# Output projection of a decoder block: from sixteen row tiles of full products to seven block products for each pair of row tiles

## The chip, the core and the metric

The kernel runs on one core of one Trainium2 chip. The metric is the device time of one execution in microseconds; for the kernel before it is 2237.41 us, the median of 3 runs (2236.44 to 2240.11).

## What is computed

One decoder layer over 2048 positions of width 1024, all in float32: a conditioned RMS norm, a combined input projection, a recurrent branch, an attention branch with three dilated windows, two branch projections that are merged with sigmoid gates, and at the end

```python
    merged = jax.nn.sigmoid(g_r + bg_r) * y_rnn + jax.nn.sigmoid(g_a + bg_a) * y_attn
    x = x + gate[:, None, :] * (merged @ w_o[l])
return rms_norm(x, g_final)
```

The change is in the last of these: `merged` (2048 x 1024) times `w_o` (1024 x 1024), with the gate on its columns, the residual add and the final norm, and in what runs just ahead of it.

## The kernel before, in words

**Precision.** TensorE multiplies operands in a rounded float32 form. Each operand is therefore split into a high part, made by a copy on ScalarE (`hi_act`, L157), and a low part, the rest, made by a subtraction on GpSimd (`lo_pool`, L163) or VectorE (`lo_dve`, L166). One product is three matmuls (`mm3`: high x high, high x low, low x high, all recorded at L149). In names of tiles, an `h` or `l` at the end is the high or low part; a weight tile `S` holds both.

**Stages.** The input projection comes first. It is done in block form already: a pair of 2 x 2 blocks takes seven products instead of eight (`strassen`, with PSUM sums X, Z, W, V, Y; each product is 4 x 3 = 12 matmuls of 128x512). Attention follows, and under it, as filler, the two branch projections: a generator, `steps` (`fill`), goes through eight jobs, four for the recurrent branch and then four for the attention branch, numbered 0 to 7 here, each with 512 positions. A job has eight output tiles m, a tile has eight steps k, a step is one `mm3`. So a job is 64 steps, 192 matmuls.

**What a step issues.** At k = 1 and k = 5 `load_w` brings a weight tile S (four buffers, each for half of a tile's depth) three half tiles ahead of its use. At k = 1 VectorE also evicts the tile before (`evict`, L1711 and L1713: the sum in PSUM times the gate gaT, plus the other branch mrT). At k = 3 `load_g` loads gaT and mrT for this tile (tiles `fg`, four buffers, 256 KB each), and at k = 7 the tile before is stored to `meT`, which is `merged` turned. The next job's left side, eight pieces `y` of 256 KB, is loaded and split around the last tile of a job, at places that the tables `LOAD_Y` and `SPLIT_Y` give (buffers R, four).

**Weights.** Earlier in the kernel both branch weights are split once and put into a scratch tensor `wD`; a tile from there is 512 KB and ready to use (`load_wd`, L339).

**The last stretch.** Jobs 0 to 5 are spent under attention, in an order written out by hand (`manual_schedule`). Jobs 6 and 7 come after it, and the order there is not by hand: the scheduler of the framework places the instructions by itself. Job 6 runs first; then `output_operands` gates and splits `w_o` into `oh` and `ol`; then `output` is called for 16 row tiles of 128 positions, and beside each of the first eight rows eight steps of job 7 are emitted. From the third tile of job 6 on, `load_w` does not use `wD`: it loads the raw 256 KB (tile `wr`) and splits it there on ScalarE and on VectorE or GpSimd (L1670 ff.). A row loads x (`xo`) and its columns of `meT` (`mraw`), splits the latter (`mh`, `ml`), makes two halves of 8 x 3 = 24 matmuls in PSUM tiles `pq`, adds each half to x (L1851), squares the row on ScalarE (L1854), works out the reciprocal root on small operands (L170 to L179), scales (L1856) and stores 512 KB (L1857).

**Queues.** All loads and stores of this stretch are issued by SyncE, in program order. Its DMAs take turns on eight semaphores, so a DMA waits for the one that was issued eight before it.

Of the kernel before, what the change touches and what calls it, by code (L numbers as in the profile page):

```python
# [10 lines left out]
F32 = mybir.dt.float32  # L11
F32R = mybir.dt.float32r
# [8 lines left out]
P = 128  # L21
# [68 lines left out]
def decoder_block(ctx, tc, x, c, positions, g_norm, w_mod, b_mod, w_in, b_gate, conv_w, conv_b,  # L90
# [60 lines left out]
    def mm3(o, lh, ll, rh, rl, first=True, last=True, **kw):  # L151
        mm(o, lh, rh, first, False, **kw)
        mm(o, lh, rl, False, False, **kw)
        mm(o, ll, rh, False, last, **kw)

    def hi_act(o, i):
        nc.scalar.activation(o, i, AF.Copy)  # L157
# [7 lines left out]
    def lo_dve(o, i, h):  # L165
        return nc.vector.tensor_tensor(o, i, h.bitcast(F32), ALU.subtract).ins  # L166
# [168 lines left out]
    def load_wd(i, m, half):  # L335
        x = n_w[0]
        n_w[0] += 1
        W[x] = t = T(pS, [P, 2, KH, P], F32R, f"S{x % 4}")
        nc.sync.dma_start(t[:].bitcast(F32), wD[i, m, half])  # L339
# [1306 lines left out]
            at(e + 1, TAIL, self.merge, 3)  # L1646
            at(e + 2, TAIL, self.store)

    stored, whole = set(), []


    def steps(jobs):

        tiles = [(j, m) for j in range(len(jobs)) for m in range(KT)]
        Y, G = {}, {}

        def load_w(x):

            if x < 2 * len(tiles):
                assert x == n_w[0]  # L1660
                j, m = tiles[x // 2]
# [4 lines left out]
                n_w[0] += 1  # L1666
                W[x] = T(pS, [P, 2, KH, P], F32R, f"S{x % 4}")
                t = T(whole[0], [P, KH, P], F32, "wr", bufs=3)
                rows = slice(x % 2 * KH * P, (x % 2 + 1) * KH * P)
                nc.sync.dma_start(t[:], (w_out_rnn, w_out_attn)[jobs[j][0]][0, rows, m * P : (m + 1) * P]  # L1670
                                  .rearrange("(k p) m -> p k m", p=P))
# [36 lines left out]

        def evict(t, ps):
            g = G[t]  # L1710
            nc.vector.tensor_tensor(g[0][:], ps[:], g[0][:], ALU.mult)  # L1711
            if len(g) > 1:
                nc.vector.tensor_tensor(g[0][:], g[0][:], g[1][:], ALU.add)  # L1713
# [99 lines left out]
    pools.close("ap", "sc", "pT", "po")  # L1813

    fp = pools.open("fp", bufs=1)
    whole.append(pools.open("wr", bufs=1))
    pq = pools.open("pq", bufs=4, space=PSUM)
    oh = T(fp, [P, KT, D], F32R, "oh")
    ol = T(fp, [P, KT, D], F32R, "ol")
    gf = T(fp, [P, D], F32, "gf")  # L1820
    nc.sync.dma_start(gf[:], g_final.unsqueeze(0).broadcast_to([P, D]))
    gate_b = T(fp, [P, D], F32, "gate_b")
    nc.sync.dma_start(gate_b[:], gateD[0:1, :].broadcast_to([P, D]))

    def output_operands():
        for k in range(KT):
            t = T(fp, [P, D], F32, "xo", bufs=2)
            nc.sync.dma_start(t[:], w_o[0, k * P : (k + 1) * P, :])
            nc.vector.tensor_tensor(t[:], t[:], gate_b[:], ALU.mult)
            hi_act(oh[:, k, :], t[:])  # L1830
            (lo_dve if k % 2 else lo_pool)(ol[:, k, :], t[:], oh[:, k, :])

    def output(n):

        for r in range(4):
            xo = T(fp, [P, D], F32, "xo", bufs=2)
            nc.sync.dma_start(xo[:], xv[n, r])
            t = T(fp, [P, KT, P], F32, "mraw", bufs=2)
            c0 = n * CH + r * P
            nc.sync.dma_start(t[:], meT[:, c0 : c0 + P].rearrange("(k p) j -> p k j", p=P))  # L1840
            th = T(fp, [P, KT, P], F32R, "mh", bufs=3)
            tl = T(fp, [P, KT, P], F32R, "ml", bufs=3)
            hi_act(th[:], t[:])
            lo_dve(tl[:], t[:], th[:])
            for q in range(2):
                cq = slice(q * CH, (q + 1) * CH)
                ps = T(pq, [P, CH], F32, "pq")
                for k in range(KT):
                    mm3(ps[:], th[:, k, :], tl[:, k, :], oh[:, k, cq], ol[:, k, cq],
                        first=k == 0, last=k == KT - 1)  # L1850
                nc.vector.tensor_tensor(xo[:, cq], ps[:], xo[:, cq], ALU.add)  # L1851
            ob = T(fp, [P, D], F32, "ob", bufs=1)
            ss = T(fp, [P, 3, 1], F32, "ss", bufs=4)
            nc.scalar.activation(ob[:], xo[:], AF.Square, accum_out=ss[:, 0])  # L1854
            rstd(ss)
            nc.vector.scalar_tensor_tensor(ob[:], xo[:], ss[:, 1], gf[:], ALU.mult, ALU.mult)  # L1856
            nc.sync.dma_start(outv[n, r], ob[:])  # L1857
            yield
# [9 lines left out]
    pools.close("wr", "fp", "pq", "fl", "pR", "pS", "pjb")  # L1868


# [27 lines left out]
```

## Time and profile before

| | us |
|---|---|
| median of 3 runs | 2237.41 |
| the profiled execution | 2235.07 |
| its span, first to last instruction | 2233.3 |
| TensorE busy | 2185.9 (98%) |
| VectorE / ScalarE / GpSimd busy | 1348.6 / 1256.2 / 978.3 |
| mean granted TensorE clock | 0.994 |
| DMA, mean over the span | 257 GB/s |

A line of an operation names the source line, the engine, the output and the inputs with their shapes, the count, and after the bar the busy time in us and the mean ns of one. The mean of a 128x512 matmul (390 ns) is longer than the distance between two of them, because they overlap; the pace has to be read from the chain of waits, where runs of matmuls stand with their count. A line of a window gives, for a stretch of the span, the busy time of each engine with its count of instructions, the granted clock, the share of time in which the DMA engines were busy, and GB/s.

### The profile page before, as it was taken

The page shows a single profiled execution, that of the slowest core. Times are in us where ns is not written, and L with a number is a line of the kernel's source. Part 1 is how long each engine was busy: PE and PEld are TensorE (multiplying, and loading weights), DVE is VectorE, ACT ScalarE, POOL GpSimd, SP SyncE. Part 2 cuts the span into 40 slices and gives each one's busy share as a digit, 9 for nine tenths or more (in the row PEclk, how much of TensorE's full clock was granted, in tenths as well). Part 3 has the DMA queues.
Part 4 walks back from the last instruction along what each step waited for, and adds up shares of the span by engine and source line. Part 5 has one row for each costly group of instructions (what it writes and reads, how often), then busy time and mean ns, then how long its engine had stood idle before and what let it go on. Part 6 is the DMA issues. An engine that isn't in the chain of part 4 may idle for free.

```text
span 2233.3 us, 33998 instructions
## 1 busy us (share of the span) xinstructions
PE 2185.9 (98%) x11422; PEld 1851.1 (83%) x11422; DVE 1348.6 (60%) x2380; ACT 1256.2 (56%) x2481; POOL 978.3 (44%) x734
## 2 busy tenths in 40 slices
PE   8999999999999999999999999999999998999998
PEld 5998888888778998888888887888888887878886
DVE  5838887878455815544545442566677777666443
ACT  6638678668543627556556202667778887533211
POOL 2457777767557422222222102455566665332100
PEclk9999999999999999999999999999999999999999
DMA  8367887887998378888888988988988887899542
GB/s 286 117 211 259 287 295 269 292 282 269 326 282 288 114 229 271 286 286 280 287 288 278 343 291 286 285 265 259 271 255 264 246 262 216 254 338 284 155 132 85
DMA packets 428626, 573.64 MB, mean 257 GB/s; under 512 B 72134, under 2 KB 292514, under 8 KB 427428
## 3 DMA queue, kind: packets, MB, share of 16 engines
q1 hardware_dynamic: 390612, 451.73, 64.9%
q10 hardware_dynamic: 37648, 119.70, 14.0%
q8 instruction: 90, 1.47, 0.3%
q14 instruction: 84, 0.69, 0.1%
q0 software_dynamic: 192, 0.05, 0.0%
HBM read 357.44 MB, written 213.91 MB: 256 GB/s over the span
## 4 chain that ended last, share of the span: by engine, by line
PE 55%; DMA 6%; DVE 3%; ACT 3%; issue 2%; POOL 2%; SPq 1%; ACTq 0%; POOLq 0%; DVEq 0%
PE pj L149 11%; PE X L149 8%; PE V L149 7%; PE pq L149 7%; PE sc L149 4%; PE W L149 4%; PE Z L149 4%; PE o L149 4%; PE Y L149 3%; PE pT L1501 1%; DMA R<-in_w_in_dram 1%; PE pg L149 1%; PE pT L1514 1%; POOL S L163 1%; DMA gaT<-ev 1%
## 5 line engine op out<-in xcount | busy, mean ns | idle before, releaser
L149 PE MATMUL pj<-yh,S 128*128 128x512 f32 x1024 | 367.8, 403 | 9.7 <-ACT yh L157 4.8
L163 POOL TENSOR_TENSOR S<-R,S 128x512 fp32r<-128x512 f32 x168 | 252.2, 1509 | 175.0 <-ACT S L157 64.9
L149 PE MATMUL V<-T,S 128*128 128x512 f32 x1344 | 324.6, 390 | 3.7 <-DVE t L450 3.5
L149 PE MATMUL X<-T,S 128*128 128x512 f32 x1344 | 324.5, 390 | 2.9 <-POOL S L163 1.9
L149 PEld LDWEIGHTS V<-T,S 128*128 128x128 f32 x1344 | 251.8, 188 | 58.4 <-DVE t L450 2.4
L149 PEld LDWEIGHTS X<-T,S 128*128 128x128 f32 x1344 | 251.4, 188 | 58.0 <-POOL S L163 2.8
L149 PEld LDWEIGHTS pj<-yh,S 128*128 128x128 f32 x1024 | 193.2, 189 | 47.8 <-ACT yh L157 6.7
L149 PE MATMUL pj<-yl,S 128*128 128x512 f32 x512 | 201.6, 394 | 6.2 <-POOL yl L163 5.1
L1417 ACT ACTIVATE pp<-pp,st 128x256 f32<-128x256 f32 (+3 forms) x256 | 133.8, 524 | 94.0 <-DVE st L1416 92.9
L163 POOL TENSOR_TENSOR S<-s,S 128x512 fp32r<-128x512 f32 x84 | 128.9, 1535 | 113.5 <-ACT S L157 68.8
L149 PE MATMUL Z<-T,S 128*128 128x512 f32 x672 | 162.0, 390 | 0.0
L149 PE MATMUL Y<-T,S 128*128 128x512 f32 x672 | 161.8, 390 | 0.0
L149 PE MATMUL W<-T,S 128*128 128x512 f32 x672 | 161.6, 389 | 0.0
L149 PEld LDWEIGHTS W<-T,S 128*128 128x128 f32 x672 | 126.0, 188 | 26.9 <-issue 0.9
L149 PEld LDWEIGHTS Y<-T,S 128*128 128x128 f32 x672 | 125.9, 188 | 26.0
L149 PEld LDWEIGHTS Z<-T,S 128*128 128x128 f32 x672 | 125.9, 188 | 26.1
L166 DVE TENSOR_TENSOR ptl<-pT,pth 128x384 fp32r<-128x384 f32 (+1 forms) x160 | 97.9, 629 | 75.6 <-ACT pth L157 73.4
L163 POOL TENSOR_TENSOR s<-R,s 128x512 fp32r<-128x512 f32 x32 | 45.9, 1434 | 198.4 <-ACT s L157 172.1
L157 ACT ACTIVATE S<-R 128x512 fp32r<-128x512 f32 x168 | 101.7, 621 | 48.1 <-DMA R<-in_w_in_dram 21.1
L908 DVE SCALAR_TENSOR_TENSOR xc<-xr,par,xc 128x512 f32<-128x512 f32 x96 | 98.5, 1026 | 45.7 <-ACT xc L902 43.5
L1481 ACT ACTIVATE pp<-pp,M 128x256 f32<-128x256 f32 (+3 forms) x256 | 118.0, 523 | 9.9 <-DVE M L1604 9.9
L1416 DVE CUSTOM_DVE_ANT_0 pp<-sc,msk 128x256 f32<-128x256 f32 (+3 forms) x256 | 104.6, 449 | 23.6 <-PE sc L149 21.3
(334 smaller groups left out, 4731.3 us busy)
## 6 DMA issues: line engine op xcount, KB each, us to landing
sD<-S ACTq DMA_DIRECT2D x196, 512.0 KB, 4.1
S<-sD SPq DMA_DIRECT2D x196, 512.0 KB, 5.0
S<-wD SPq DMA_DIRECT2D x100, 512.0 KB, 5.4
R<-in_w_in_dram SPq DMA_DIRECT2D x136, 256.0 KB, 4.3
wD<-s ACTq DMA_DIRECT2D x64, 256.0 KB, 5.0
T<-in_w_mod_dram SPq DMA_DIRECT2D x8, 1024.0 KB, 12.0
vN<-ev SPq DMA_DIRECT2D x64, 128.0 KB, 2.7
zaT<-ev SPq DMA_DIRECT2D x32, 256.0 KB, 4.4
```

The costliest lines, as they stand in the source:

```text
L149: nc.tensor.matmul(o, lhsT=l, rhs=r, start=st, stop=sp, **kw)
L157: nc.scalar.activation(o, i, AF.Copy)
L163: nc.gpsimd.tensor_tensor(o, i, h.bitcast(F32), ALU.subtract)
L166: return nc.vector.tensor_tensor(o, i, h.bitcast(F32), ALU.subtract).ins
L908: nc.vector.scalar_tensor_tensor(xc, xr[:, i : i + CH], cw(i), xc, ALU.mult, ALU.add)
L1416: nc.vector.tensor_tensor_reduce(pdst, s_ps, mask, 1.0, 3e38, ALU.add, ALU.min, m_)
L1417: nc.scalar.activation(pdst, pdst, AF.Exp, bias=m_, scale=-1.0, accum_out=l_)
L1481: nc.scalar.activation(pp, pp, AF.Copy, scale=w)
L1501: nc.tensor.transpose(pt[:, c0 + j * P : c0 + (j + 1) * P], pp[i][:, k * P : (k + 1) * P], ident)
L1514: nc.tensor.transpose(pt[:, c * P : (c + 1) * P], pp[:, half * P : (half + 1) * P], ident)
```

## The change

`load_w` always loads the split tile from `wD`, also in jobs 6 and 7:

```diff
-                if not whole or j == NB + 2 and m < 2:
-                    load_wd(jobs[j][0], m, x % 2)
-                    return
...
-                hi_act(W[x][:, 0], t[:])
-                (lo_dve if x % 2 else lo_pool)(W[x][:, 1], t[:], W[x][:, 0])
+                load_wd(jobs[j][0], m, x % 2)
```

The output projection is written in block form. Two row tiles of 128 positions, cut into two halves of the depth, stand against `w_o` cut into 2 x 2 blocks of 512 x 512. Seven right operands (`B11`, `T2`, `T3`, `T1`, `B21`, `T4`, `B22`, each 4 x 128x512, high and low) are built once from the gated rows of `w_o`; `build_rows(s, k)` spreads this, for one of four depth pieces k, over the steps s to s + 19 of jobs 6 and 7. Per piece: two gatings of 128x1024 on GpSimd, four differences on VectorE, seven high parts on ScalarE, four low parts on VectorE and three on GpSimd.

```diff
-    spend(fill, KT * KT, 0)
-    output_operands()
-    for n in range(NB):
-        for _ in output(n):
-            for _ in range(KT):
-                next(fill, None)
+    with tc.manual_schedule():
+        v["gate"] = stage(0, [P, D])
+        nc.sync.dma_start(v["gate"][:], gateD[0:1, :].broadcast_to([P, D]))
+        load_rows(0)
+        for k in range(KH):
+            build_rows((8, 32, 72, 96)[k], k)
+            if k:
+                on((16, 44, 75)[k - 1], load_rows, k)
+        on(LAST - 24, load_left, 0)
...
+        for s in range(LAST):
+            next(fill)
+            fire(s)
...
+        load_rows_x(0)
+        load_rows_x(1)
+        nc.sync.dma_start(v["gf"][:], g_final.unsqueeze(0).broadcast_to([P, D]))
+        fire_p()
+        for p in range(NP):
+            output_pair(p)
```

`LAST` is 128: jobs 6 and 7 now run through without a break, all 384 matmuls, and then come eight pairs p of seven products. `load_rows(k)` brings two 512 KB rows of `w_o` into two of five staging tiles; `gateD` is another 512 KB. For each pair, `load_left` brings two 512 KB tiles of `meT`, `left_events` make four sums and differences on VectorE and seven split operands (ScalarE; four low parts on VectorE, three on GpSimd), four products ahead of their use. `output_pair` writes the products in this order, with their sums:

```diff
+        product(p, 0, X, "B11", True, False)
+            last_output(p - 1)
+        product(p, 1, Z, "T2", True, True)
+        product(p, 2, W_, "T3", True, True)
+        product(p, 3, V, "T1", True, False)
+            product(p, 4, X, "B21", False, True)
+        product(p, 5, Y, "T4", True, True)
```

`last_output` is the seventh product (`B22`, on V). A product is 12 matmuls. VectorE makes u2 = Z + X and u3 = W + u2 and the four sums with x from PSUM, GpSimd adds u2 and u3 to x in three pieces, and each row is squared, scaled and stored as before, some products later. In the last pair the product with `T4` comes ahead of that with `B21`, the first row is squared in two halves, and its two halves of 256 KB are scaled and stored by ScalarE and by VectorE with SyncE. The whole stretch, from the start of job 6 to the end, is in an order written by hand.

More of the change, by code (lines that the diff above doesn't have):

```diff
@@ L1833, in output @@
[L1833 to L1858, printed above, removed]
@@ L1861, in decoder_block, with stage @@
-    spend(fill, KT * KT, 0)
-    output_operands()
-    for n in range(NB):
-        for _ in output(n):
-            for _ in range(KT):
-                next(fill, None)
-    pools.close("wr", "fp", "pq", "fl", "pR", "pS", "pjb")
+    px_ = pools.open("px", bufs=1, space=PSUM)
+    for name in ("B11", "T2", "T3", "T1", "B21", "T4", "B22"):
+        B[name] = [T(fp, [P, KH, CH], F32R, name + l) for l in "hl"]
+    def stage(i, shape, dt=F32):
+        return T(fp, shape, dt, f"st{i}")
+    pend = {}
@@ new lines, in on, with fire, load_rows, gate_rows @@
+    def on(n, fn, *args):
+        pend.setdefault(n, []).append((fn, args))
+    def fire(n):
+        for fn, args in pend.pop(n, ()):
+            fn(*args)
+    v = {}
+    tt = nc.vector.tensor_tensor
+    def load_rows(k):
+        for i in range(2):
+            v[k, i] = t = stage(1 + i + 2 * (k % 2), [P, D])
+            nc.sync.dma_start(t[:], w_o[0, (k + i * KH) * P : (k + i * KH + 1) * P, :])
+    def gate_rows(k, i):
+        nc.gpsimd.tensor_tensor(v[k, i][:], v[k, i][:], v["gate"][:], ALU.mult)
@@ new lines, in part, with difference, high @@
+    def part(name, k):
+        name = {"T3": "B12", "T4": "B21"}.get(name, name)
+        if name[0] == "T":
+            if (name, k) not in v:
+                v[name, k] = T(fp, [P, KH, P], F32, {"T1": "s1", "T2": "s2"}[name])
+            return v[name, k][:].rearrange("p k j -> p (k j)")
+        i, j = int(name[1]) - 1, int(name[2]) - 1
+        return v[k, i][:, j * CH : (j + 1) * CH]
+    def difference(name, k, a, b):
+        tt(part(name, k), part(a, k), part(b, k), ALU.subtract)
+    def high(name, k):
+        hi_act(B[name][0][:, k, :], part(name, k))
@@ new lines, in decoder_block, with load_left, left @@
+    A, ops = {}, {}
+    NP = 2 * NB
+    def load_left(p):
+        for half in range(2):
+            shape = [P, KH, 2 * P]
+            A[p, half] = t = T(up[0], shape, F32, f"A{half}", bufs=2) if p else stage(1 + half, shape)
+            nc.sync.dma_start(t[:], meT[half * KH * P : (half + 1) * KH * P, p * 2 * P : (p + 1) * 2 * P]
+                              .rearrange("(k p) j -> p k j", p=P))
+    def left(p, name):
+        if name in ("s1", "s2"):
+            return v[name][:]
+        i, j = int(name[1]) - 1, int(name[2]) - 1
+        return A[p, j][:, :, i * P : (i + 1) * P]
@@ new lines, in left_sum, with left_split @@
+    def left_sum(p, dst, a, b, op):
+        if dst[0] == "s" and (dst, p) not in v:
+            v[dst, p] = v[dst] = T(fp, [P, KH, P], F32, dst)
+        tt(left(p, dst), left(p, a), left(p, b), op)
+    def left_split(p, i, name):
+        x = 7 * p + i
+        r = x % 7
+        t = T(pS, [P, 2, KH, P], F32R, f"S{r - 3}") if r > 2 else stage((3, 4, 0)[r], [P, 2, KH, P], F32R)
+        ops[x] = t
+        hi_act(t[:, 0], left(p, name))
+        (lo_pool if i % 2 else lo_dve)(t[:, 1], left(p, name), t[:, 0])
@@ new lines, in decoder_block, with load_rows_x, cols, square @@
+    XO, SS = {}, {}
+    def load_rows_x(p):
+        n, r = divmod(2 * p, 4)
+        for i in range(2):
+            XO[p, i] = t = T(up[0], [P, D], F32, "xo", bufs=4)
+            nc.sync.dma_start(t[:], xv[n, r + i])
+    def cols(p, i, j):
+        return XO[p, i][:, j * CH : (j + 1) * CH]
+    def square(p, i, js=(0, 2)):
+        if (p, i) not in SS:
+            SS[p, i] = T(up[0], [P, 3, 1], F32, "ss", bufs=4)
+        jk = T(up[0], [P, D], BF16, "jk", bufs=1)
+        c = slice(js[0] * CH, js[1] * CH)
+        nc.scalar.activation(jk[:, c], XO[p, i][:, c], AF.Square, accum_out=SS[p, i][:, 2 if js == (0, 1) else 0])
@@ new lines, in finish_row, with product @@
+    def finish_row(p, i, last=True):
+        n, r = divmod(2 * p, 4)
+        ss, t = SS.pop((p, i)), XO.pop((p, i))
+        if last:
+            rstd_last(ss)
+        nc.vector.scalar_tensor_tensor(t[:], t[:], ss[:, 1], v["gf"][:], ALU.mult, ALU.mult)
+        nc.sync.dma_start(outv[n, r + i], t[:])
+    up, n_p, psum = [], [0], {}
+    def product(p, i, ps, b, first, last):
+        bh, bl = B[b]
+        s = ops.pop(7 * p + i)
+        for k in range(KH):
+            mm3(ps[:], s[:, 0, k, :], s[:, 1, k, :], bh[:, k, :], bl[:, k, :],
+                first=first and k == 0, last=last and k == KH - 1, skip_group_check=True)
+        n_p[0] += 1
```

157 lines of the change are left out of this document (135 added, 22 removed).

## The prediction, made blind

> **What bounds the kernel now.** I read the page's first part, then the chain of waits from its end backwards, then windows over the last stretch.
>
> ```profile
> PE 2185.9 (98%) x11422; PEld 1851.1 (83%) x11422; DVE 1348.6 (60%) x2380; ACT 1256.2 (56%) x2481; POOL 978.3 (44%) x734
> ```
>
> TensorE sets the span. What counts is the pace of its matmuls, and the chain gives it:
>
> ```profile
> 1004.85 2.72 PE X L149 x12
> ...
> 2132.52 5.44 PE pj L149 x24
> 2137.96 87.05 PE pq L149 x384
> ...
> 2225.03 0.70 DVE xo L1851
> ...
> 2225.81 1.16 ACT ob L1854 x2
> ...
> 2228.38 1.28 DVE ob L1856
> ```
>
> (The first row is of the chain in the block products of the input projection, asked for by itself; the others are of the last 100 us.) 384 matmuls in 87.05 us are 226.7 ns each; a block product of 12 takes 2.72 us, the same pace. The last matmul is issued out by 2225.0; the tail to the span's end, 2233.3, is 8.3 us.
>
> ```profile
> 1950.00:2050.00 100.00, 96.42 (x423) 77.95 (x423) 69.82 (x79) 38.06 (x55) 37.52 (x22) 1.00 0.99 314
> 2060.00:2225.00 165.00, 165.00 (x728) 136.32 (x727) 64.21 (x132) 29.55 (x52) 7.07 (x3) 1.00 0.41 134
> ```
>
> So the last stretch (jobs 6 and 7 and the output) has two parts: up to 2050 TensorE loses 3.6 us while the DMA engines are busy 0.99 of the time, and after it TensorE has no gap and DMA is at 0.41. What it waits for in the first part is DMA, one transfer behind the other:
>
> ```profile
> 1956.77 6.92 DMA S<-wD
> ...
> 1963.76 7.16 DMA fg<-mrT
> ...
> 1970.96 7.01 DMA xo<-in_w_o_dram
> ```
>
> The stretch has 2 x 192 matmuls of the jobs and 16 x 48 = 768 of the output, 1152 in all: 1152 x 0.2267 = 261.2 us, with the 3.6 us 264.8 us. Counted back from 2225.0 it begins near 1960.
>
> **The change, part by part.**
>
> *Products.* 8 pairs x 7 x 12 = 672 matmuls take the place of 768. At 226.7 ns the 96 are worth 21.8 us, and all of it is on the path. The stretch's floor becomes 1056 x 0.2267 = 239.4 us.
>
> *DMA beside jobs 6 and 7.* This is the term that decides. Before, job 7 was spread between output rows, so its loads had 24 + 48 matmuls to hide under; and most weight tiles were 256 KB. Now both jobs run through: 384 x 0.2267 = 87.1 us. In this time must land: 30 of the 32 weight tiles of 512 KB (two are on their way), 32 loads of gaT and mrT and 16 stores of 256 KB, 8 pieces y of job 7 of 256 KB, 8 rows of `w_o` and the gate of 512 KB, and two left tiles of 512 KB. That is 15360 + 8192 + 4096 + 2048 + 4096 + 512 + 1024 = 35328 KB, 36.2 MB; in 87.1 us, 415 GB/s. What DMA has reached when it was busy all the time:
>
> ```profile
> 1260.00:1270.00 10.00, 9.68 (x43) 7.71 (x42) 5.24 (x10) 2.85 (x5) 0.85 (x1) 1.00 1.04 396
> 1270.00:1280.00 10.00, 10.00 (x45) 8.26 (x45) 6.94 (x9) 1.14 (x3) 4.23 (x4) 1.00 1.02 399
> ...
> 1930.00:1940.00 10.00, 10.00 (x67) 8.86 (x66) 6.66 (x10) 4.84 (x10) 3.23 (x2) 1.00 1.02 346
> 1940.00:1950.00 10.00, 10.00 (x68) 9.05 (x67) 4.88 (x8) 4.11 (x8) 3.83 (x3) 1.00 1.03 337
> 1960.00:1970.00 10.00, 8.82 (x39) 6.90 (x38) 3.00 (x4) 0.00 (x0) 1.16 (x1) 1.00 1.02 383
> 1970.00:1980.00 10.00, 7.99 (x35) 5.97 (x34) 4.43 (x5) 3.70 (x5) 3.39 (x3) 1.00 1.08 349
> ```
>
> None reaches 415, so TensorE must wait for bytes. 399 is a window that consists nearly of large reads; 314 is the mean of 1950 to 2050 above, with small runs in it. The four windows between have just these loads, weight tiles, y, gaT, mrT and stores, and their mean is 354. I take 355: 36.2 MB / 355 GB/s = 102 us, **+14.9 us** of waiting. Bounds: 399 gives 90.7 us, +3.6; 314 gives 115.3 us, +28.2.
>
> Where it shows: a weight tile is asked for when its buffer is free, three half tiles (3 x 2.72 = 8.2 us) ahead of use. Rows of issues, the last number being the us to landing:
>
> ```profile
> S<-wD SPq DMA_DIRECT2D x100, 512.0 KB, 5.4
> ...
> fg<-mrT SPq DMA_DIRECT2D x32, 256.0 KB, 5.2
> ...
> R<-oT SPq DMA_DIRECT2D x28, 256.0 KB, 6.2
> ...
> xo<-in_w_o_dram SPq DMA_DIRECT2D x8, 512.0 KB, 5.8
> ```
>
> 5.4 us leave 2.8 us of room, which is two 512 KB transfers ahead in the queue (1.5 us each at 355 GB/s). The first weight tile behind the gate and two rows of `w_o` has three ahead; so has the one at step 44 with two rows and a y. The last pieces y are loaded 9 steps (6.1 us) ahead of use, and landing alone is 6.2. These three places should show stalls of 2 to 4 us; they are how the 14.9 us appear, not more on top. SyncE is in order too: mrT takes the buffer that VectorE's second addition frees, so its load waits there, with weight tile and store queued behind.
>
> *Splits taken out.* 28 raw weight tiles go, and the output's own operands:
>
> ```profile
> L157 ACT ACTIVATE S<-wr 128x512 fp32r<-128x512 f32 x22 | 13.7, 628 | 30.7 <-DMA wr<-in_w_out_attn_dram 21.3 <-PE pj L149 9.1
> ...
> L163 POOL TENSOR_TENSOR S<-wr,S 128x512 fp32r<-128x512 f32 x11 | 17.2, 1565 | 40.6 <-ACT S L157 40.5
> L163 POOL TENSOR_TENSOR ol<-xo,oh 128x1024 fp32r<-128x1024 f32 x4 | 10.2, 2553 | 15.7 <-ACT oh L157 13.0 <-issue 2.7
> ...
> L166 DVE TENSOR_TENSOR S<-wr,S 128x512 fp32r<-128x512 f32 x11 | 10.9, 997 | 2.7 <-ACT S L157 2.7
> L1713 DVE TENSOR_TENSOR fg<-fg,fg 128x512 f32<-128x512 f32 x12 | 10.7, 891 | 7.6 <-DMA fg<-mrT 7.6
> L1711 DVE TENSOR_TENSOR fg<-pj,fg 128x512 f32<-128x512 f32 x12 | 8.2, 683 | 3.4 <-DMA meT<-fg 1.7 <-DMA fg<-gaT 0.9 <-PE pj L149 0.8
> ```
>
> None of these engines sets the end, so I credit nothing beyond the old 3.6 us.
>
> *Right operands built.* ScalarE 28 x 0.63 = 18 us, VectorE 16 x 0.89 + 16 x 1.0 = 30 us, GpSimd 12 x 1.57 + 8 x 2.55 = 39 us, beside 102 us. With the evictions, 16 x (0.68 + 0.89) = 25 us, VectorE is at 55 of 102. I cost it at nothing: the cover is the matmuls of both jobs, the last piece is done by step 115 of 128. Without cover one piece would add about 20 steps, 13.6 us.
>
> *Start of the products.* Four x rows, the final weights and the second pair's two left tiles, 3584 KB = 3.7 MB, are issued only after the last store of job 7: eviction 1.6 us, 10.3 us at 355 GB/s, 2 us to land, then on VectorE a sum, and a split, 0.89 + 0.63 + 1.0: 16.4 us. The second pair's first operand is needed after six products, 6 x 2.72 = 16.3 us. **+1 us**, between 0 and 4.
>
> *Products after that.* VectorE has per pair four sums, four low parts, six evictions, two scalings and small operations (1.4 us per row, between the chain's 1.16 and 1.28 rows): 3.6 + 4.0 + 4.1 + 2.6 + 2.8 = 17.1 us of 7 x 2.72 = 19.0. Off the path, with two products of slack in every PSUM sum: 0. At a tenth more it still fits.
>
> *Clock.* A long wait lowers the granted clock:
>
> ```profile
> 1866.87 0.50 PE L149 MATMUL pj<-yh,S 128*128 128x512 f32 x1 [1.35 <-ACT yh L157]
> 1870.44 0.79 PE L149 MATMUL pj<-yl,S 128*128 128x512 f32 x1 [3.08 <-POOL yl L163]
> ```
>
> ```profile
> 1870.00:1880.00 10.00, 9.55 (x44) 8.65 (x45) 4.28 (x9) 3.44 (x11) 3.42 (x3) 0.68 0.32 104
> ```
>
> After these two the clock was 0.68 over 10 us, 3.2 us lost; in 1970 to 1980, with 2.0 us of shorter gaps, it stayed at 1.00. One or two of the stalls above are of the long kind, partly inside DMA waiting anyway: **+2 us**, between 0 and 6. The Trainium skill, "TensorE: Matmul & The Clock Gate", Part 1, has the clock halve after an idle window of about 3.4 us; by it stalls of 2 to 3 us would cost nothing and this term would be 0. The trace is against it as a threshold: a gap of 3.08 us was enough here.
>
> *Tail.* The last row is squared in two halves and scaled in halves on two engines: from 1.16 and 1.28 us about 0.35 and 0.6 go, the last store is 256 KB instead of 512 KB (0.4 less at most), one small addition comes in: **-1.1 us**, between -2 and 0. The other row's scaling (1.28 us) and two 128x512 operations lie under the last product, 2.72 us.
>
> *Sum.* 239.4 + 14.9 + 1 + 2 = 257.3 us for 264.8: -7.5; with the tail, and a rounding up for restarts after gaps (0.11 us each in the 0.50 row, some ten): -7.4. From the profiled 2235.07 that is 2227.7 us. The profiled execution lies 2.34 us under the median, so for the median **2230 us**.
>
> **The rivals.**
>
> *Slower, by DMA.* If the stage gets the 314 GB/s of 1950 to 2050, jobs 6 and 7 take 115.3 us; with 3 us at the start of the products and 5 us of clock: 239.4 + 28.2 + 8 = 275.6, +10.8, with the tail +9.7: 2247 us. It decides against the change below 330 GB/s (109.7 us). For it: stores and loads mixed, and DMA behind in-order waits of SyncE. Against: the windows of the same mix at 337 to 383, though only one of them is below 346.
>
> *No wall.* At the 399 of the best window, 90.7 us, nothing at the start and no long stall: 239.4 + 3.6 = 243.0, -21.8, with the tail -22.9: 2214 us. For it: nearly half the bytes are 512 KB weight tiles and rows, as in that window. Against: half are not. The Trainium skill, "HBM Reference", Specifications, says that a core streaming alone measures about 425 GB/s; no window here shows that, the best being 399. By it the 36.2 MB would take about 85 us, an estimate from that page, and there would be no wait at all.
>
> *VectorE binds the products.* If contention makes its 17.1 us per pair 20, each pair gains 1 us: +8 us, 2238 us. For it: it is in order, and holds left operands, evictions and rows. Against: uncontended 128x512 operations are 0.68 to 0.70.
>
> **How the numbers follow.** Forecast (337 to 385 GB/s) 0.55; slower by DMA 0.22; no wall 0.12; VectorE 0.11. Such a measurement tells about 0.2% (4.5 us) from no change. Faster by more: rates above about 344 GB/s, most of the forecast and the second rival, 0.59. Within: rates from 319 to 344 and most of the third, 0.21. Slower: 0.20. The range is 2219 (385 GB/s, nothing lost elsewhere) to 2243 (320 GB/s); about one in ten lies on either side.
>
> **What would show it.** In the profile after: 24 matmuls of a job in well over 5.44 us, DMA share near 1 and 340 to 370 GB/s for about 100 us from 1960; stalls behind `S<-wD` near the first `w_o` rows and at step 44, and at the last y pieces of job 7; then eight pairs at 19.0 us without gaps; a tail of about 7 us. It is wrong if job time is 87 us, if the products show waits on VectorE or GpSimd, or if DMA is below 0.95 while TensorE waits (then it is SyncE's order, not bytes).

## The result, and the profile after

The changed kernel takes 2241.53 us (median of 20 runs, 2235.32 to 2246.81), the kernel before beside it on the same chip 2237.30 us (20 runs). The ratio is 1.0018, 95% interval 1.0011 to 1.0025: 4.2 us slower where 7.4 us faster was forecast. The profiled execution took 2239.79 us, its span is 2238.0.

The page of the changed kernel answers the line of the engines first:

```profile
PE 2171.1 (97%) x11326; PEld 1834.1 (82%) x11326; DVE 1403.2 (63%) x2452; ACT 1267.8 (57%) x2524; POOL 1054.7 (47%) x784
```

96 matmuls are gone, as planned, and TensorE is busy 14.8 us less. Its span is longer all the same, so idle time took their place. Windows over the stretch show where: first the kernel before, cut where its last matmul of job 7 ends, then the changed kernel, cut at the same event (columns: window, length, busy time and count of TensorE, its weight loads, VectorE, ScalarE, GpSimd, then granted clock, DMA share, GB/s).

```profile
1958.70:2105.00 146.30, 142.72 (x624) 116.15 (x623) 88.71 (x122) 47.19 (x71) 41.48 (x23) 1.00 0.85 271
2105.00:2225.00 120.00, 120.00 (x530) 99.06 (x528) 45.97 (x96) 19.47 (x35) 0.75 (x1) 1.00 0.36 117
```

```profile
1961.00:2074.30 113.30, 96.11 (x385) 74.20 (x383) 57.78 (x74) 23.86 (x39) 44.97 (x26) 0.94 0.91 322
2074.30:2228.70 154.40, 153.11 (x673) 125.74 (x671) 129.06 (x214) 53.78 (x108) 70.17 (x47) 1.00 0.45 158
```

Before, jobs 6 and 7 were spread among 240 matmuls of the output: 146.3 us, with a loss of 3.6 us. Now they run through. Their 384 matmuls need 384 x 226.7 ns = 87.1 us and take 113.7 (1960.8 to 2074.5, by the first and last matmul). The products after them take 154.2 us for a floor of 672 x 226.7 ns = 152.3, and the tail from the last matmul to the end is 9.3 us for 8.3. In all 277.2 us stand against 266.5 + 8.3 = 274.8: +2.4 us. (The rest of the difference between the two spans lies ahead of job 6, where both kernels issue the same instructions; that start falls anywhere between 1957 and 1968 us in the profiles of this study, so I compare lengths of stages, not spans.)

The 26.6 us lost in the jobs are of two kinds: TensorE is idle for 113.3 - 96.1 = 17.2 us of the window, and busy for 96.1 us where 87.1 would do. The waits of TensorE in the jobs (what waited, for what: us in total, times, longest):

```profile
PE pj L149 <- DMA S<-wD: 10.2, 4, 5.2
PE pj L149 <- DVE s L1842: 3.7, 4, 1.6
PE pj L149 <- ACT yh L157: 1.7, 2, 1.3
PE pj L149 <- POOL yl L163: 0.8, 1, 0.8
```

The second row is a wait for weight tiles too. In each of its four cases a weight tile had landed 0.13 to 0.14 us before the matmul, and in three of them the weight load of that matmul began before VectorE's sum, to which the row puts the wait down, had ended. The first case, with a tile that landed at 1994.92:

```profile
1994.37 0.68 DVE L1842 TENSOR_TENSOR s<-st 128x512 f32<-128x512 f32 x1
```

```profile
1995.03 0.19 PEld L149 LDWEIGHTS pj<-yh,S 128*128 128x128 f32 x1 [1.96 <-DVE fg L1702]
```

So some 14 of 17 us are a wait for weight tiles. Why they are late is in the queue's own waits, those of SyncE in the same stretch:

```profile
SPq L1695 <- DMA fg<-mrT: 24.5, 11, 4.0
SPq L1695 <- DVE fg L1702: 15.1, 14, 2.4
SPq L339 <- PE pj L149: 14.8, 9, 4.6
```

In the first two rows SyncE stands 39.6 us at line 1695, where `load_g` issues the loads of gaT and mrT, and only 14.8 us at line 339, where it waits for a weight buffer. The chain of waits names the loop (start, us, what):

```profile
1973.84 4.50 DMA fg<-mrT
...
1978.44 0.70 DVE fg L1702
1979.16 7.25 DMA fg<-mrT
...
1986.50 1.99 DVE fg L1702
...
2002.70 9.57 DMA S<-wD
```

A load of mrT goes into the buffer that VectorE's addition (line 1702) has just freed, and that addition waits for the load of mrT before it: 14 of the last 17 loads of mrT are issued within 0.1 us of the end of such an addition, in the kernel before one of 17. One transfer at a time is under way on this path, and SyncE, in order, holds every weight tile, piece y and store behind it. At the end a weight tile is issued at 2002.7, lands 9.57 us later, behind a piece y and two rows of `w_o`, and TensorE stands for 5.2 us. This is the place at step 44 that the prediction had named, with 2 to 4 us. What that does to the clock is seen in windows of 10 us:

```profile
2000.00:2010.00 10.00, 6.50 (x28) 4.74 (x26) 6.79 (x9) 2.50 (x4) 2.46 (x2) 1.00 0.87 310
2010.00:2020.00 10.00, 7.59 (x24) 6.13 (x25) 2.59 (x4) 2.03 (x4) 1.82 (x2) 0.66 0.99 379
2020.00:2030.00 10.00, 7.22 (x24) 4.83 (x24) 2.90 (x4) 2.39 (x4) 4.45 (x3) 0.86 0.96 330
2030.00:2040.00 10.00, 10.00 (x37) 8.10 (x36) 6.43 (x8) 2.60 (x5) 6.03 (x4) 0.80 0.83 261
```

In the last of these TensorE is busy throughout and gets through 37 matmuls instead of 44, at a clock of 0.80. In the three windows below full clock TensorE is busy 24.8 us for 85 matmuls, which need 19.3: 5.5 us.

The DMA engines have idle time, but hardly any while TensorE waits. In the long wait they are full; what they did not use lies ahead of it:

```profile
1996.00:1998.00 2.00, 2.00 (x10) 1.62 (x10) 0.46 (x1) 0.00 (x0) 1.09 (x1) 1.00 0.49 111
2002.00:2006.00 4.00, 4.00 (x19) 3.27 (x18) 3.64 (x5) 1.34 (x3) 1.74 (x1) 1.00 0.67 188
2007.20:2012.40 5.20, 0.01 (x1) 0.02 (x1) 0.96 (x2) 0.63 (x1) 1.26 (x1) 0.78 1.03 409
```

### The profile page after: what moved, and what is told of

The parts are those of the page before. It is cut to its first block, busy times and chain, and to the rows that moved or that the text cites. A ratio compares the mean times of both kernels' runs of the same rounds, so it can differ in the third digit from the quotient of the medians.

```text
span 2238.0 us, 33996 instructions
## 1 busy us (share of the span) xinstructions
PE 2171.1 (97%) x11326; PEld 1834.1 (82%) x11326; DVE 1403.2 (63%) x2452; ACT 1267.8 (57%) x2524; POOL 1054.7 (47%) x784
## 5 line engine op out<-in xcount | busy, mean ns | idle before, releaser
L149 PE MATMUL pj<-yh,S 128*128 128x512 f32 x1024 | 372.3, 408 | 21.8 <-DMA S<-wD 10.6
L163 POOL TENSOR_TENSOR S<-s,S 128x512 fp32r<-128x512 f32 x92 | 139.7, 1519 | 116.5 <-ACT S L157 73.0
```

The source lines that it names most:

```text
L149: nc.tensor.matmul(o, lhsT=l, rhs=r, start=st, stop=sp, **kw)
L163: nc.gpsimd.tensor_tensor(o, i, h.bitcast(F32), ALU.subtract)
```

## The experiments

**Theory L** (the loop): SyncE's order, with the load of mrT waiting for the load before it, keeps the DMA engines from being used. **Theory B** (bytes): 36.2 MB need this time at the rate that the mixture gets, whatever their order. After the first batch a third candidate came in, **the turn** from job 6 to job 7 with its eight pieces y. Each experiment has one profile, from which the stage lengths are; the ratios are to the kernel before, run on the same chip (the changed kernel itself: 1.0018).

| run | us | ratio, 95% interval | jobs 6, 7 | products | tail |
|---|---|---|---|---|---|
| changed kernel | 2241.53 | 1.0018 [1.0011, 1.0025] | 113.7 | 154.2 | 9.3 |
| e1 mrT in idle buffers | 2235.01 | 0.9982 [0.9970, 0.9995] | 106.7 | 153.9 | 9.3 |
| e2 half of the weights' bytes | 2231.00 | 0.9968 [0.9955, 0.9981] | 100.1 | 155.3 | 9.3 |
| e3 earlier places | 2242.19 | 1.0019 [1.0008, 1.0030] | 113.7 | 155.5 | 9.3 |
| e5 e1 with e2 | 2229.42 | 0.9948 [0.9930, 0.9965] | 100.6 | 154.4 | 9.3 |
| e7 e1, store later | 2232.96 | 0.9974 [0.9961, 0.9986] | 105.8 | 154.2 | 9.3 |
| e8 e7, other tail | 2234.67 | 0.9975 [0.9964, 0.9985] | 103.8 | 155.0 | 9.6 |
| e9 no pieces of job 7 | 2238.99 | 1.0000 [0.9985, 1.0014] | 109.5 | 155.1 | 9.3 |
| e10 e5 with e9 | 2223.93 | 0.9934 [0.9918, 0.9951] | 94.8 | 154.5 | 9.3 |
| e11 e7 with e9 | 2226.26 | 0.9935 [0.9921, 0.9949] | 96.7 | 154.5 | 9.3 |
| e12 e7 with e3 | 2235.50 | 0.9981 [0.9971, 0.9991] | 108.2 | 153.6 | 9.3 |
| e13 18 raw weight tiles | 2242.95 | 1.0015 [1.0004, 1.0025] | 112.8 | 155.6 | 9.3 |
| e14 e13 with e7 | 2246.68 | 1.0039 [1.0025, 1.0053] | 117.2 | 154.9 | 9.4 |

Two more edit the kernel before: e4 (2243.32 us, 1.0019 [1.0009, 1.0029]) and e6 (2238.68 us, 0.9993 [0.9982, 1.0004]). The products (153.6 to 155.6) and, but for e8, the tail are the same in all of them; the jobs are what moves. e7 and e8 have the same jobs and differ by 2.0 us there, so differences of 2 us between two profiles tell nothing.

### e1: the loop taken away

For 11 of the 16 tiles the load of mrT gets a buffer of its own, one that is idle while no piece y is loaded.

```diff
-                g = T(fl, [P, CH], F32, "fg", bufs=4)
+                if src is mrT and (j == NB + 2 and m < 5 or j == NB + 3 and m > 1):
+                    g = T(pR, [P, CH], F32, f"R{m % 4}")
+                else:
+                    g = T(fl, [P, CH], F32, "fg", bufs=4)
```

> The changed kernel with one edit: in 11 of the 16 tiles of jobs 6 and 7, mrT is loaded into one of the four buffers R, which stand empty then, instead of the one buffer that VectorE's second addition has to free. Bytes and arithmetic are the same. In the changed kernel jobs 6 and 7 took 113.3 us, and SyncE stood 40 us of it at the load of mrT (24.5 us put down to the mrT before, 15.1 us to VectorE's addition). Theory L (the loop of mrT, addition, next mrT, with the weight tile queued behind it on SyncE): jobs 6 and 7 fall to what the bytes allow, 36.2 MB at 355 GB/s = 102 us, DMA share 0.98 or more, the whole 2230 us (-11). Theory B (bytes at the rate that this mix gets, 320 GB/s): jobs 6 and 7 stay at 111 to 115 us, the whole 2240 to 2243 us.

Measured: the jobs take 106.7 us, 7.0 less, and the time falls below that of the kernel before. The window of the jobs has DMA at 0.96 for 0.91. SyncE's waits where mrT is loaded, for mrT and for the addition, fall from 39.6 us to 8.2; a store that waits for VectorE's sum stands first instead (the edit moves the line numbers by 3):

```profile
1957.40:2064.10 106.70, 94.17 (x386) 73.45 (x385) 58.56 (x74) 23.97 (x40) 45.47 (x26) 0.97 0.96 344
```

```profile
SPq L1710 <- DVE fg L1705: 14.9, 7, 3.7
```

The loop is a cause, shown, and worth 7 us of the 26.6. The long wait near step 44 falls from 5.2 to 2.7 us with it.

### e2: half of the bytes

The weight tiles of both jobs load only their high part (256 KB), which stands in for the low part too; the low part of these weights is left out of the sums.

```diff
+        if half_tile:
+            nc.sync.dma_start(t[:, 0].bitcast(F32), wD[i, m, half, :, 0])
...
```

> The changed kernel with the weight tiles of jobs 6 and 7 cut to their high part: 256 KB instead of 512 KB each; the third matmul of a step uses the high part again, so the low part of these weights is left out of the result. Matmuls and waits are the same in number; 30 x 256 KB = 7.9 MB less. Theory B: 28.3 MB at 320 GB/s = 88 us, so jobs 6 and 7 are bound by TensorE's 87.1 us and take about 89; the whole 2217 us. Theory L: the loop stays. A tile took 7.1 us; without one of the two large transfers ahead of mrT its landing is about 1 us sooner, so 6.1 us x 16 = 98 us; the whole 2226 us.

Measured: 100.1 us, 13.6 less, where theory B had 89 and theory L 98. Theory B alone falls: with 8.4 MB fewer the DMA engines are at 0.85, and TensorE still loses 13 us. The 13.6 us are not the price of the bytes alone, since the loop turns faster too: SyncE stands 26.9 us in it for 39.6.

```profile
1965.10:2065.20 100.10, 93.15 (x386) 74.44 (x385) 61.73 (x74) 23.92 (x40) 46.17 (x26) 0.95 0.85 285
```

### e3: earlier places

The last three pieces y of job 7 and the rows of `w_o` are asked for some steps earlier, and five pieces are split one or two steps earlier.

```diff
+    LOAD_7 = {-12: 0, -10: 1, -8: 2, -6: 3, -2: 4, 2: 5, 3: 6, 4: 7}
+    SPLIT_7 = {-3: 0, 1: 1, 2: 2, 3: 3, 6: 4, 9: 5, 10: 6, 12: 7}
...
-                on((16, 44, 75)[k - 1], load_rows, k)
+                on((13, 30, 67)[k - 1], load_rows, k)
```

> The changed kernel with only places in the written order moved: the last three pieces y of job 7 are loaded two steps earlier (and pieces 1, 2, 4, 5, 6 split one or two steps earlier), and the rows of w_o for depth pieces 1, 2, 3 at steps 13, 30, 67 instead of 16, 44, 75, so that the second of them does not fall into the loads of y. Same bytes. If the stalls at single places are what costs (5.2 us at the weight tile behind w_o and y, 2.8 us at the last pieces y, and the lower clock after them, about 6 us): jobs 6 and 7 fall by 6 to 12 us, the whole 2230 to 2235 us. Theories B and L: the work only moves, 113 us within 3, the whole 2239 to 2243 us.

Measured: 113.7 us as before the edit. SyncE stands 22.7 us for mrT and 13.6 us for VectorE at the same line. These earlier places gain nothing while the loop holds the queue.

### e4: the weights part alone

In the kernel before, all weight tiles of jobs 6 and 7 are loaded split; the output stays as it was, spread among the jobs.

```diff
-                if not whole or j == NB + 2 and m < 2:
+                if True:
```

> The kernel before with one part of the change alone: all weight tiles of jobs 6 and 7 are loaded split (512 KB) instead of 28 raw tiles of 256 KB that are split on the chip. The output stays as it was, job 7 spread between its rows. 7.3 MB more, 28 splits less. Theory B: of the 28 tiles 12 lie in job 6, where DMA was busy 0.99 of the time: 3.1 MB at 330 GB/s = +9.5 us there, less 2 us of waits for splits; the rest lies where DMA is at 0.41: the whole 2244 us. If loading the weights split costs nothing by itself: 2235 to 2238 us.

Measured: the whole stretch 269.4 us for 266.5, the time 0.19% longer. With 146 us for the two jobs, loading the weights split still costs about 3 us, where the expectation had 9.5 less 2 for the splits. TensorE waits 5.7 us for weight tiles, in the kernel before 1.2 and 2 more for splits of weight tiles.

### e5: loop and bytes together

The edits of e1 and e2 in one kernel (the low part of the weights left out).

> Both earlier edits in one: mrT of 11 of the 16 tiles of jobs 6 and 7 goes into idle buffers, and the weight tiles of these jobs load only their high part (the low part of these weights is left out of the sums). Jobs 6 and 7 took 113.7 us with neither, 106.7 with the first, 100.1 with the second; their 384 matmuls need 87.1. If loop and bytes are two causes beside each other, the gains add up to 20.6 us: jobs in 90 to 95 us, the kernel at 2220 to 2225. If the loop only hurts because the bytes fill the DMA engines (one cause), lifting it after the bytes are halved brings nothing: jobs again at 98 to 101 us, the kernel at 2231.

Measured: 100.6 us, the second outcome. Once the bytes are halved, taking the loop away brings nothing that the profile shows; by the jobs, the two are not terms to be added. The times are less clear: 0.9948 lies below e2's 0.9968, the intervals overlap, and the sum of both gains, 0.9932, lies inside e5's. Between 2000 and 2030 this kernel still gets only 86 matmuls through, which need 19.5 us: 10.5 us are lost there, at the turn, and only some 3 us elsewhere.

```profile
2000.00:2030.00 30.00, 23.62 (x86) 17.55 (x85) 13.43 (x16) 7.86 (x13) 12.77 (x9) 0.89 0.83 269
```

### e6: the loop in the kernel before

The edit of e1 in the kernel before the change.

> The kernel before the change, with the same loads of mrT moved to idle buffers. If the loop at mrT costs only where the split weights fill the queue behind it, nothing comes of it: within 0.1% of the kernel before (its stretch is 266.5 us, of which 1152 matmuls need 261.2, so at most 5 us are there to be had). If the loop costs TensorE in any kernel, the stretch falls to 262 or 263 us and the time to 2233.

Measured: 0.9993, no difference that can be told. The run does not show that the loop is harmless in this kernel, for the kernel before has no such loop to take away. SyncE does stand at the same loads there, but until a store has landed; the waits for mrT and for the addition come to 1.7 us (kernel before, from job 6 to job 7's last matmul):

```profile
SPq L1706 <- DMA meT<-fg: 30.4, 9, 5.3
...
SPq L1706 <- DMA fg<-mrT: 0.9, 1, 0.9
...
SPq L1706 <- DVE fg L1713: 0.8, 1, 0.8
```

The loop came in with the change, which writes the order of this stretch by hand; what in that order makes it was not tested.

### e7 and e8: SyncE's next wait, and the tail

e7 is e1 with the store of a tile moved behind the next tile's weight load.

```diff
-                if k == 7 and t:
-                    store(t - 1)
+                if k == 7 and 0 < t <= (NB + 2) * KT:
+                    store(t - 1)
+                if k == 2 and t > (NB + 2) * KT + 1:
+                    store(t - 2)
...
+        store(len(tiles) - 2)
```

> mrT in idle buffers, and the store of a tile of jobs 6 and 7 issued behind the next tile's weight load, by when VectorE has long finished its sum: SyncE stood 14.9 us at these stores in the run with the mrT loads alone (7 times, longest 3.7 us). If it is the order on SyncE that still holds TensorE, jobs 6 and 7 fall from 106.7 us to 100 to 103 and the time to 2230 (0.9965). If the rate of the DMA engines is what is left (their share was 0.96 at 344 GB/s, and 36.2 MB at 344 to 355 GB/s are 102 to 105 us), the jobs stay at 105 to 107 and the time at 2235 (0.998).

Measured: 105.8 us, within what two profiles differ by from e1; the second outcome. SyncE's wait at the stores falls from 14.9 to 5.8 us, and DMA stays at 0.96, with 347 GB/s.

e8 adds to it a shorter tail: row 1's reciprocal root behind the sums of squares of row 0, and one product with the final weights on GpSimd.

```diff
             square(p, 1)
-            rstd_first(SS[p, 1])
-            rstd_last(SS[p, 1])
             row_start()
             fire_p()
             square(p, 0, (0, 1))
+            rstd_first(SS[p, 1])
+            rstd_last(SS[p, 1])
+            nc.gpsimd.tensor_tensor(cols(p, 0, 0), cols(p, 0, 0), v["gf"][:, :CH], ALU.mult)
             finish_row(p, 1, False)
-            tt(cols(p, 0, 0), cols(p, 0, 0), v["gf"][:, :CH], ALU.mult)
             last_output(p)
```

> As the run with the moved store, and in the last pair row 1's reciprocal root and the product of row 0's first half come behind the sums of squares of row 0 and on GpSimd, so that VectorE is free when the last product ends (it came 1.8 us late in the profile after). The tail from the last matmul to the end falls from 9.3 us to 7.5 to 8, and the time by 1 to 2 us against the run with the moved store. If the tail is set by ScalarE's squares and the store's landing instead, it stays at 9.3 us.

Measured: the tail is 9.6 us, neither 7.5 to 8 nor the 9.3 of the other outcome. The timeline of e8 tells why (start, us, engine, line):

```profile
2222.24 1.28 POOL L2040 TENSOR_TENSOR xo<-xo,gf 128x512 f32<-128x512 f32 x1 [4.46 <-ACT jk L1937]
...
2222.48 1.06 DVE L176 TENSOR_TENSOR ss<-ss 128x1 f32<-128x1 f32 x1
...
2224.15 1.28 DVE L1944 SCALAR_TENSOR_TENSOR xo<-xo,ss,gf 128x1024 f32<-128x1024 f32 x1
2225.35 0.68 DVE L1963 TENSOR_TENSOR xo<-V,xo 128x512 f32<-128x512 f32 x1
```

The last matmul ended at 2223.3; the sum with V (line 1963) starts 2.0 us later, behind the root, one step of which took 1.06 us while GpSimd multiplied, and behind row 1's scaling of 1.28 us. My edit moved the root onto the path instead of off it.

### e9, e10, e11: the turn taken away

Job 7 multiplies by the split pieces of job 6; its own eight are neither loaded nor split, and are left out of the result. e9 does this alone, e10 with e5 (the low part of the weights left out too), e11 with e7.

```diff
+                elif j1 == NB + 3:
+                    if x in SPLIT_Y:
+                        Y[j1, SPLIT_Y[x]] = Y[j, SPLIT_Y[x]] if j < j1 else Y[j - 1, SPLIT_Y[x]]
...
-                if j1 and x in SPLIT_Y:
+                if j1 and j1 != NB + 3 and x in SPLIT_Y:
```

> Kernel after, but job 7 multiplies by the split pieces of job 6: its eight attention pieces are neither loaded (2.1 MB, eight loads on SyncE) nor split, which leaves them out of the result. In the 30 us around the turn from job 6 to job 7 the profile after has 75 matmuls, which need 17.0 us: 13.0 us are lost there; with loop lifted, bytes halved or both it is still 11.6, 10.3 and 10.5. If the turn is a cause of its own, jobs 6 and 7 fall from 113.7 us to 101 to 104 and the time to 2229 (0.995). If the turn is only where the shortage of bytes comes to light, the 2.1 MB are 6 us at 344 GB/s and the stalls come elsewhere: jobs at 107 to 109 us, the time at 2235.

> All three lifted: mrT in idle buffers, only the high part of the weight tiles (the low part left out), no pieces of job 7 (job 6's used again). The 384 matmuls need 87.1 us. If loop, bytes and turn are the whole of the 26.6 us, the jobs take 88 to 91 us and the kernel 2220 (0.991). If something else holds TensorE (the building of the right operands, the clock), they stay at 96 to 100 us and the time at 2227 to 2229.

> Full weight tiles, mrT in idle buffers, the store behind the next weight load, and no pieces of job 7 (left out, job 6's used again). 105.8 us of jobs with the pieces, of which 11.9 were lost around the turn. If the turn is a cause of its own: 94 to 97 us, the kernel at 2223 (0.993). If bytes bind: (36.2 - 2.1) MB at 347 GB/s = 98.3 us and more, 98 to 101 us, the kernel at 2227.

Measured: alone 109.5 us, 4.2 less, near the second outcome; with the loop taken away too 96.7 us, in the first range; with all three 94.8 us, between the two outcomes written down. The waits of TensorE and SyncE in e9 show that the loop is still there: 12.1 us behind weight tiles, SyncE again at mrT.

```profile
PE pj L149 <- DMA S<-wD: 12.1, 7, 3.5
```

```profile
SPq L1695 <- DMA fg<-mrT: 35.9, 15, 4.2
```

e11 has all weights in full, and TensorE waits for weight tiles alone, 5.5 us. Here DMA has little room left, at 0.98 and 358 GB/s, and SyncE mostly waits for weight buffers, as it should:

```profile
1958.80:2055.50 96.70, 91.05 (x386) 72.54 (x385) 55.80 (x70) 18.99 (x32) 40.56 (x22) 0.98 0.98 358
```

```profile
SPq L339 <- PE pj L149: 20.7, 15, 2.6
```

```profile
PE pj L149 <- DMA S<-wD: 5.5, 6, 2.0
```

So the 355 GB/s of the forecast is a rate that these loads reach without the pieces y, when SyncE is seldom held. That bytes alone set what is still lost in e11 is not shown: e10, with 8.4 MB fewer, is only 1.9 us shorter. It has the store where e1 has it, and SyncE stands there 11.7 us. The loop is worth 12.8 us without the pieces (e9 to e11, the store with it), 7.9 with them (changed kernel to e7), nothing that its profile shows with half the bytes.

### e12: the places again, without the loop

e7 with the places of e3.

> mrT in idle buffers, the store behind the next weight load, and the last pieces of job 7 and the w_o rows loaded and split at earlier steps (which alone gave nothing: 1.0019, the loop holding SyncE). If the places of the pieces set the turn, the 11.9 us lost there fall to 6 or 8: jobs 100 to 102 us, the time at 2229 (0.995). If the turn is set by the buffers (a piece is split when job 6 has read its last matmul of the piece before it) or by the rate, it stays at 105 to 106 us and 2233 (0.9974).

Measured: 108.2 us, no gain over e7, a little above the second outcome. TensorE now waits longest for the low part of a piece y:

```profile
PE pj L149 <- DVE yl L166: 7.2, 3, 5.0
```

ScalarE had made the high part of that piece by 2018.9. On VectorE, which works in order, the low part stands behind the eviction of a tile, and that waited for gaT, which landed at 2020.5, and then for mrT:

```profile
2020.61 0.69 DVE L1703 TENSOR_TENSOR fg<-pj,fg 128x512 f32<-128x512 f32 x1 [4.89 <-issue]
2023.05 0.69 DVE L1705 TENSOR_TENSOR fg<-fg,fg 128x512 f32<-128x512 f32 x1 [1.75 <-DMA fg<-mrT]
2023.66 0.68 DVE L166 TENSOR_TENSOR yl<-R,yh 128x512 fp32r<-128x512 f32 x1
```

### e13 and e14: the weights part undone

In the changed kernel 18 of the 32 weight tiles of the jobs (tiles 2 to 5 of job 6, 3 to 7 of job 7) are loaded whole, 256 KB, and split on the chip half a tile ahead. e14 has this with e7.

```diff
+                R[x] = t = T(pR, [P, CH], F32, f"R{x % 4}")
...
+                hi_act(W[x][:, 0], w)
+                (lo_dve if x % 2 else lo_pool)(W[x][:, 1], w, W[x][:, 0])
```

> Part of the weights' change undone in the changed kernel, nothing left out: 18 of the 32 weight tiles of jobs 6 and 7 (tiles 2 to 5 of job 6, 3 to 7 of job 7) are loaded whole (256 KB instead of 512 KB) into the idle buffers and split on the chip half a tile ahead, by ScalarE and by VectorE or GpSimd. That is 4.7 MB less of 36.2. Halving all 32 tiles took 13.6 us off the jobs, so by bytes 13.6 x 18/32 = 7.6: jobs 105 to 107 us, the time 2234 (0.9975). If the splits cost what the loads save (18 more ScalarE, 9 more VectorE and 9 more GpSimd instructions where the right operands are being built), TensorE waits for S from ScalarE or GpSimd instead: jobs 110 to 115 us, the time 2240 to 2243 (1.000 to 1.002).

> The same 18 raw weight tiles with mrT in idle buffers and the store behind the next weight load (two of the four buffers for each). Lifting the loop on top of halved bytes gave nothing (100.1 and 100.6 us), so by the one-queue theory the jobs are at 101 to 104 us here and the time at 2229 to 2231 (0.996); nothing is left out, so this is the candidate that should beat the kernel before. If the raw loads hold the two buffers against each other or the splits bind: 106 us or more, 2233 to 2238.

Measured: 112.8 us, the second outcome. e14 is the slowest of all with 117.2 us and 2246.68, beyond both outcomes written down for it. DMA has room in e13 (0.86), but the waits went over to the engines. The waits of TensorE, then those of ScalarE, in e13:

```profile
1964.20:2077.00 112.80, 96.37 (x385) 72.22 (x385) 81.86 (x83) 32.70 (x57) 62.31 (x35) 0.97 0.86 283
```

```profile
PE pj L149 <- POOL S L163: 4.4, 7, 1.1
```

```profile
ACT S L157 <- DMA R<-in_w_out_attn_dram: 35.3, 9, 13.4
ACT B11h L157 <- POOL st L1852: 10.6, 3, 4.0
```

ScalarE, in order, stands up to 13.4 us for a raw tile, and the pieces y and the right operands stand behind it. In this order and in these buffers, which the pieces y use as well (in e14 mrT too), 18 raw tiles cost as much as split ones. That the split load costs nothing does not follow (e4).

## Why the prediction was wrong

The changes of the ratio against the changed kernel agree with those of the jobs in the profiles: e10 0.84% of 2240 us, 18.8 us, for 18.9 in the jobs; e9 4.0 for 4.2; e1 8.1 for 7.0; e2 11.2 for 13.6; the others on this kernel agree within 3 us too.

*Products* was right: 96 matmuls less, and 7 products per pair. *Start of the products* and *Products after that* were right too: 154.2 us for 152.3 + 1. The rival in which VectorE binds the products did not come.

***DMA beside jobs 6 and 7* is the step that failed.** The bytes were right (113.3 us at 322 GB/s are 36.5 MB, for 36.2 forecast), and the rate was near (347 GB/s in e7 with all loads, 358 in e11 without the pieces y). That is in part luck: two of the four windows behind the 355, from 1960 to 1980, hold more than the loads named there, the final weights, the gate, raw weight tiles, rows of `w_o` and columns of `meT` among them. What failed is the sentence that the stalls are "how the 14.9 us appear, not more on top". It treats the queue as if it always had a transfer to do. It had not: DMA was at 0.91 over the jobs, and at 0.67 from 2002 to 2006, ahead of the longest wait. This is near the sign that the prediction had written down for SyncE's order, DMA below 0.95 while TensorE waits, but not that sign: in the wait itself DMA was at 1.03. The idle time comes first and the wait after it, which fits transfers that were held back and then stood in the queue together. The prediction even named the wait, mrT in the buffer that VectorE's addition frees, with weight tile and store behind it, and gave it no price. The jobs took 113.7 us for 102 + 2, 9.7 more. e1 shows 7.0 of this to be the loop. Without it, and with the stores moved (e7), the jobs take 105.8 us, 1.8 over the forecast, which is no more than two profiles differ by. That does not make every part of the forecast right. The eight pieces at the turn to job 7 cost 9.1 us once the loop is gone (e7 to e11, 105.8 to 96.7), their splits included, where their 2.1 MB at 355 GB/s are 5.9.

*Splits taken out* and *Right operands built*, both at nothing, hold for the changed kernel: the 3.7 us put down to VectorE's sums end with weight tiles, and TensorE waits 1.7 + 0.8 us for the splits of y, which may stand behind the building. e13 shows how near the limit this was.

*Clock*, priced at 2 us, was under-sized: three windows alone show 5.5 us. I had counted it as partly hidden under waits for DMA. A slow TensorE frees buffers later, and in the window with clock 0.80 and no wait DMA fell to 0.83; that the bytes lost there come back later as waits is argued from this window, not shown by an experiment.

*Tail* had the wrong sign: +1.0 for -1.1. "The other row's scaling and two 128x512 operations lie under the last product" did not hold. The timeline of the changed kernel (the last matmul, of `V<-B22h`, ends at 2228.7):

```profile
2228.62 1.28 DVE L1938 SCALAR_TENSOR_TENSOR xo<-xo,ss,gf 128x1024 f32<-128x1024 f32 x1
...
2229.82 0.68 DVE L2035 TENSOR_TENSOR xo<-xo,gf 128x512 f32<-128x512 f32 x1
...
2230.42 0.68 DVE L1957 TENSOR_TENSOR xo<-V,xo 128x512 f32<-128x512 f32 x1
```

Row 1's root came only when the product had nearly ended, so its scaling and one more operation stand in front of the sum with V, 1.7 us after the matmul.

Put together: jobs 113.7 for 104, +9.7; products 154.2 for 153.3, +0.9; tail +2.1; less 1.7 us that the old stretch was longer than the 264.8 of the forecast, and the 1.2 us that had been added for restarts: 9.8 us, from -7.4 to +2.4 in the stretch. The rival that came nearest is *Slower, by DMA*: 115.3 us of jobs at 314 GB/s, where 113.7 at 322 was measured. Its reason was only half right, since the engines were not full over the stage; it had named SyncE's in-order waits as well.

Of the versions with nothing left out, e7 is the fastest by its median: 2232.96 us, 0.26% under the kernel before and 0.44% under the changed one. e8, e1 and e12 lie close behind it. Most of the gain that was sought, 5.8 of 7.4 us, is there once SyncE's queue is kept moving.

## What to carry to other kernels

When work is moved together so that one stage must run at the rate of its transfers, price the stage by the order of the queue as well as by its bytes: look for a load that takes a buffer which a computation frees only after that load's own predecessor has landed, and count everything behind it. Such a loop need not be there in the old order (one load of mrT in 17 was in it) and can cost 7 to 13 us in the new one. Causes that share one queue need not add: in the profiles the loop and the pieces y took 7.9 and 4.2 us off the jobs alone and 17.0 together. Take them away one at a time and all together before you put a price on any of them.

## What the runs showed of the hardware

The granted clock fell after gaps that were short one by one. In e5 TensorE stood 2.38, 0.23, 0.19 and 0.85 us within 6 us, and the clock of the window around the last of these was 0.66 (the first row is the first gap, from the timeline; the second is the window):

```profile
2018.96 0.50 PE L149 MATMUL pj<-yh,S 128*128 128x512 f32 x1 [2.38 <-ACT yh L157]
```

```profile
2020.00:2030.00 10.00, 8.97 (x26) 6.53 (x25) 5.45 (x5) 3.61 (x6) 8.04 (x5) 0.66 0.70 221
```

The Trainium skill, "TensorE: Matmul & The Clock Gate", Part 1, names an idle window of about 3.4 us. The trace does not bear that out as a threshold: in e11 a single gap of 2.03 us, the only one between 2018 and 2033, was followed by a clock of 0.50 from 2027 to 2030, which makes 0.84 over 10 us:

```profile
2025.43 0.47 PE L149 MATMUL pj<-yh,S 128*128 128x512 f32 x1 [2.03 <-DMA S<-wD]
```

```profile
2020.00:2030.00 10.00, 7.97 (x29) 6.08 (x29) 6.91 (x8) 2.49 (x4) 5.82 (x3) 0.84 1.02 403
...
2027.00:2030.00 3.00, 3.00 (x9) 2.32 (x8) 2.04 (x2) 0.63 (x1) 3.00 (x2) 0.50 1.02 397
```

An operation of VectorE on 128x1 took 1.06 us beside a GpSimd multiplication of 128x512 (e8, above), where its neighbours on VectorE took 0.15 to 0.16. It ended with the multiplication, at 2223.5.
